# A hybrid decoder step on one core: the memory attention of the sample tokens is paced by other numbers, and the first memory weight tile is rounded in a later call

## The chip, the core and the metric

The kernel runs on one core of a Trainium2 chip. The metric is device time in microseconds (us) of one execution. Three executions of the kernel before took 1181.36, 1183.0 and 1184.02 us. A profile of a further execution shows what each engine did: PE (TensorE, matmuls), PEld (its weight loads), DVE (VectorE), ACT (ScalarE), POOL (GpSimd) and SP, whose queue issues the DMAs.

## The reference

One step of a decoder layer for a prompt of 1024 tokens and eight sample tokens, with shared weights. One input projection feeds three groups of heads: a Mamba-2 state-space group, a dilated window attention, and a cross-attention over 256 memory tokens. Their gated outputs go through one output projection, a residual add and a norm. The part that matters here is the cross-attention, for the prompt with freshly projected memory, for the sample tokens with a cache:

```python
def memory_kv(mem, mem_norm_g, w_mem_kv):
    m = rms_norm(mem, mem_norm_g)
    kv = jnp.einsum('bmd,dn->bmn', m, w_mem_kv)
    k, v = jnp.split(kv, 2, axis=-1)
    return heads(k, CROSS_HEADS), heads(v, CROSS_HEADS)

def cross_attend(q, k, v):
    scale = q.shape[-1] ** -0.5
    sc = jnp.einsum('bthe,bmhe->bhtm', q.astype(F32), k.astype(F32)) * scale
    p = jax.nn.softmax(sc, axis=-1)
    return jnp.einsum('bhtm,bmhe->bthe', p, v.astype(F32))
```

## The kernel before

Products of float32 numbers are made of rounded parts: each operand is split in a high part (`h`, a cast on ACT) and a low part (`l`, a subtraction on DVE or POOL; `split`, L69 to L78), and three matmuls replace one.

The stages in order: q, k and v for all tokens by token tiles (`token_tile`), the memory's keys and values (`memory_tile`, eight tiles of `w_mem_kv`, in between the value tiles), the cross-attention's queries and gates by feature tiles (`feature_tile`: 128 output features, all tokens in three chunks, 24 matmuls each), the prompt's cross-attention, the window attention, the state-space part, and the output projection. `fslot` loads a weight tile of 512 KB into `raw`, one of two buffers, and splits it.

The order of PE's instructions is written out by hand, those of the other engines (and of SP's queue) by a scheduler. PE's order comes from generators that `step` advances: each matmul group yields a cost in ns, and `spend` adds it to a clock, `now`. Background generators are advanced when that clock has passed what they yielded last. `settle` (called at the end of the cross-attention stage, before its buffers are given back) runs whatever the background still holds at once, with no other matmul between.

One background generator is `samples`: the sample tokens' window attention, and then their memory attention, both in `sample_attention`. Of the memory attention (names ending in m: `prm`, `ktm`), for each of eight tokens and two sets of 128 memory rows, a key tile `kt` is loaded (L390), multiplied with the query on DVE (L391) and reduced per head (L392); each of these 16 steps yields 2100 ns, and 6000 ns follow. Then the scores are transposed on PE (`sTm`, L399), the softmax is made, its result transposed back (`sPm`, L432), and 16 value tiles of 256 KB are multiplied on PE (`som`, L464) in four groups of four. Value tiles share five buffers with the key tiles: the first five are loaded ahead, the others as each group gives its buffers back (`load_v`, L449). After each half DVE masks the results (L474), and `sfom` (L480, eight small products in float32) sums them; its first half needs only the first masks.

In the program around it PE works at four gate tiles (`gates`, names `gc`) and then at tiles of z. A gate's end is ACT's tanh (L349), DVE's product (L350), POOL's product with the attention result (L355), and a store of 512 KB to `cat_d` (L358) on SP.

Of the kernel before, what the change touches and what calls it, by code (L numbers as in the profile page):

```python
# [12 lines left out]
F32R = mybir.dt.float32r  # L13
# [7 lines left out]
P = 128  # L21
# [4 lines left out]
KT = D // P  # L26
# [10 lines left out]
def hybrid_step(ctx: ExitStack, tc: tile.TileContext, i, o):  # L37
# [14 lines left out]
    def bank(tag, name):  # L52
        return phase["pool"].tile([P, 512], F32, tag=tag, name=name, bufs=phase["bufs"][tag])
# [10 lines left out]
    def late(ins):  # L64

        if hold:
            after(hold[0], ins)

    def as32(ap):  # L69
        return ap.bitcast(F32)  # L70

    def split(h, l, src, hi=ACT, lo=POOL, mid=None):

        if hi is ACT:
            ACT.copy(h, src)  # L75
        else:
            hi.tensor_copy(h, src)
        lo.tensor_tensor(l, src, as32(h), op=ALU.subtract)  # L78
# [13 lines left out]
    def open_pool(name, side="left"):  # L92
        guards[name] = tc.tile_pool(name=name, bufs=1, side=side, reuse_waits="tile")
        return guards[name].__enter__()
# [77 lines left out]
    def product():  # L172

        return next(x for x in reversed(nc.cur_bb.bb.instructions) if x.engine == mybir.EngineType.PE)

    def after(product, ins):

        sync = mybir.DependencyInfo(mybir.DependencyClass.Sync, mybir.DependencyReason.DATA)
        tc.add_manual_dep(ins.ins, product.name, sync, reason="pace")
# [9 lines left out]
    w2_ = open_pool("w2", "right")  # L189
# [26 lines left out]
    def wslot(name, cols, start=None, pieces=range(4)):  # L216
        out = []
        for j in pieces:
            off, src = 0, []
            for c0, n in cols:  # L220
                src.append((i["w_in"][256 * j:256 * j + 256, c0:c0 + n], off))
                off += n
            out.append(wpiece(f"{name}{j}", src, off, start))
        return out

    def tok_major(ps, slot, xh, xl, n=512, middle=None):


        for kt in range(KT):
            if kt == KT // 2 and middle:  # L230
                middle()
            wh, wl = (t[:, kt % 2, :n] for t in slot[kt // 2])
            PE.matmul(ps, lhsT=xh(kt), rhs=wh, start=(kt == 0), stop=False)  # L233
            PE.matmul(ps, lhsT=xh(kt), rhs=wl, start=False, stop=(kt == KT - 1 and not xl))  # L234
            if xl:
                PE.matmul(ps, lhsT=xl(kt), rhs=wh, start=False, stop=(kt == KT - 1))
            spend(640.0 if xl else 427.0)

    low = [DVE]

    def fslot(name, c0, n=P, w=None, start=None):

        raw = w2_.tile([P, KT, P], F32, tag="fraw", name="raw_" + name, bufs=2)[:, :, :n]
        load = SP.dma_start(raw, (i["w_in"] if w is None else w)[:, c0:c0 + n].rearrange("(k p) n -> p k n", p=P))
        if start:
            after(start, load)
        h = w2_.tile([P, KT, P], F32R, tag="fwh", name="wh_" + name, bufs=2)[:, :, :n]
        l = w2_.tile([P, KT, P], F32R, tag="fwl", name="wl_" + name, bufs=2)[:, :, :n]
        split(h, l, raw, lo=low[0])
        return h, l  # L250

    q_d = dram.tile([S, 512], F32, tag="q_d", name="q_d")

# [62 lines left out]
    def rope(out, x, n, c, s, eng):  # L316

        t = xp_.tile([P, 4, 8, 8], F32, tag="ropet", name="ropet")[:n]
        cb, sb = (v.unsqueeze(1).to_broadcast([n, 8, 8]) for v in (c, s))
        x1, x2 = x[:, :, 0:8], x[:, :, 8:16]  # L320
        eng.tensor_tensor(t[:, 0], x1, cb, op=ALU.mult)
        eng.tensor_tensor(t[:, 1], x2, sb, op=ALU.mult)
        eng.tensor_tensor(t[:, 2], x2, cb, op=ALU.mult)
        eng.tensor_tensor(t[:, 3], x1, sb, op=ALU.mult)
        eng.tensor_tensor(out[:, :, 0:8], t[:, 0], t[:, 1], op=ALU.subtract)
        eng.tensor_tensor(out[:, :, 8:16], t[:, 2], t[:, 3], op=ALU.add)

    def feature_tile(name, c0, done, m=P, lead=0):


        def work(wh, wl):
            for c in range(3):
                cs = slice(c * CH - (lead if c else 0), (c + 1) * CH)
                ps = bank("acc", f"{name}_{c}")[:m, :cs.stop - cs.start]
                for kt in range(KT):
                    PE.matmul(ps, lhsT=wh[:, kt], rhs=hTh[:, kt, cs], start=(kt == 0), stop=False)  # L336
                    PE.matmul(ps, lhsT=wl[:, kt], rhs=hTh[:, kt, cs], start=False, stop=False)  # L337
                    PE.matmul(ps, lhsT=wh[:, kt], rhs=hTl[:, kt, cs], start=False, stop=(kt == KT - 1))  # L338
                    if kt == KT - 1:
                        done(ps, c, cs)  # L340
                    yield 437.0
        add(name, lambda: fslot(name, c0, m), lambda slot: work(*slot))
# [35 lines left out]
    def sample_attention(b_, name, H, sets, q_rows, rows_k, rows_v, scale, new, out):  # L378
# [6 lines left out]
        for b in range(NB):  # L385
            qb = wide("qb", 2)
            SP.dma_start(qb, q_rows[b:b + 1].to_broadcast([P, 512]))
            for s_ in range(sets):
                kt, pr = wide("kt", 5), wide("pr", 2)
                late(SP.dma_start(kt, rows_k(b, s_)))  # L390
                DVE.tensor_tensor(pr, kt, qb, op=ALU.mult)  # L391
                DVE.tensor_reduce(sc[:, s_, b], pr.rearrange("p (h d) -> p h d", h=H), axis=AX.X, op=ALU.add)  # L392
                yield 2100.0
        yield 6000.0
        W = sets * P + (NB if new else 0)
        st = t_([R, W], "st")
        for s_ in range(sets):
# [19 lines left out]
        mx, l, r = t_([R, 1], "mx"), t_([R, 1], "l"), t_([R, 1], "r")  # L417
# [38 lines left out]
        for g in range(2):  # L456
            POOL.memset(om[g], 0.0)
            for s_ in range(sets):
                if s_ == 0:
                    ob = bank("o", f"so{name}{g}")  # L460
                n = 4 * (g * sets + s_)
# [37 lines left out]
    def samples():  # L499
        yield from sample_attention(sa_, "w", 8, 3, qs_d, win(wk), win(wv), 0.125, (o["win_k_s"], o["win_v_s"], 3.0), oAs)  # L500
        while "qc3" not in finished:
            yield 1000.0
        yield from sample_cross(sa_)
# [7 lines left out]
    def join(out, ps, low):  # L511

        DVE.tensor_copy(out[:2 * NB], ps[:2 * NB])
        SP.dma_start(low, out[NB:2 * NB])
        DVE.tensor_tensor(out[:NB], out[:NB], low, op=ALU.add)

    def token_tile(name, T, out, row, middle=None):
        n = P if T < NT else NB
        cs = slice(T * P, T * P + n)
        ps = bank("acc", f"{name}{T}")  # L520
        t = xp_.tile([P, 512], F32, tag="qkv", name=f"{name}sb{T}", bufs=2)
        if T < NT:
            tok_major(ps, slot, lambda kt: hTh[:, kt, cs], lambda kt: hTl[:, kt, cs], middle=middle)
            DVE.tensor_copy(t, ps)
        else:
            tok_major(ps[:2 * NB], slot, lambda kt: hTs[:, kt], None)
            join(t, ps, xp_.tile([P, D], F32, tag="xsq", name=f"{name}low")[:NB, :512])
            t = t[:NB]
        if name != "v":
            c, s = (cos[:, T], sin[:, T]) if T < NT else (cos_s, sin_s)  # L530
            v = t.rearrange("p (h d) -> p h d", h=8)
            rope(v, v, n, c, s, POOL)
        SP.dma_start(out[cs] if T < NT else row, t)
        finished.add(f"{name}{T}")

    def memory_tile(f, slot):
        wh, wl = slot
        ps = bank("acc", f"mem{f}")[:, :256]
        for kt in range(KT):
            PE.matmul(ps, lhsT=wh[:, kt], rhs=mth[:, kt], start=(kt == 0), stop=False)  # L540
            PE.matmul(ps, lhsT=wl[:, kt], rhs=mth[:, kt], start=False, stop=False)
            PE.matmul(ps, lhsT=wh[:, kt], rhs=mtl[:, kt], start=False, stop=(kt == KT - 1))
        t = xp_.tile([P, 512], F32, tag="qkv", name=f"mkv{f}", bufs=2)[:, :256]
        DVE.tensor_copy(t, ps)
        SP.dma_start(o["mem_k" if f < 4 else "mem_v"][:, f % 4], t)
        spend(2600.0)
# [73 lines left out]
    for T in (0, NT, *range(1, NT)):  # L620
        token_tile("k", T, o["win_k"], o["win_k_s"])
        if T == 5:
            start = product()
        if T == 0:
            norm_start("m1")
        elif T in (2, 4):
            norm_end(f"m{T // 2 - 1}")
    slot = wslot("v", [(C_V, 512)])
    mem_w = [fslot("m0", 0, w=i["w_mem_kv"], start=start)]
    for T in (0, NT, *range(1, NT)):  # L630
        token_tile("v", T, o["win_v"], o["win_v_s"])
        if T < NT:
            if T < NT - 1:
                mem_w.append(fslot(f"m{T + 1}", P * (T + 1), w=i["w_mem_kv"], start=product()))
            memory_tile(T, mem_w.pop(0))
# [957 lines left out]
```

## Time and profile before

| what | value |
|---|---|
| median of three executions | 1183.0 us (1181.36 to 1184.02) |
| the profiled execution | 1182.3 us, its span 1180.5 us |
| busy in the span | PE 1107.3, PEld 950.8, DVE 720.1, ACT 477.8, POOL 393.7 us |
| moved by DMA | 137.45 MB, mean 116 GB/s |
| mean granted PE clock | 0.987 of full speed |

The span is the time from the first to the last instruction that the profiler shows. Idle time of an engine counts only where it lies on the chain that ends last. All durations below come from the one profiled execution.

### The profile page before, as it was taken

To read this page: it belongs to the slowest core of one execution; us is meant where nothing else is said; L and a number is where in the kernel's file an instruction comes from. 1 tells how busy PE (TensorE), PEld (TensorE's weight loads), DVE (VectorE), ACT (ScalarE), POOL (GpSimd) and SP (SyncE) were. 2 spreads that over 40 slices of the span, in tenths; PEclk is the share of its full clock that TensorE was granted. 3 is DMA by queue.
4 is the path that set the end of the run, shared out by engine and by line. 5 is a ranking of instruction groups with operands and counts; after the bars stand their busy time and mean duration, and the time that the engine had idled before them with its cause. 6 is when DMAs were issued, how large, how long until landed. Compare 5 with 4: busy or idle time off the path is not lost.

```text
span 1180.5 us, 19065 instructions
## 1 busy us (share of the span) xinstructions
PE 1107.3 (94%) x7059; PEld 950.8 (81%) x7059; DVE 720.1 (61%) x1524; ACT 477.8 (40%) x1156; POOL 393.7 (33%) x422
## 2 busy tenths in 40 slices
PE   7999999999899999999999999998997898998987
PEld 5867676898888888878888899998997777776865
DVE  5558632358842657566664286877858856375663
ACT  5320110244422666565654133555544645214121
POOL 2355200000134205143323411554534325361871
PEclk9999999999999999999999899999998999999999
DMA  5658547613547422121201321112213333363732
GB/s 196 216 162 262 155 117 210 196 45 113 156 143 207 130 76 88 39 76 55 76 21 44 116 93 39 36 41 69 76 51 99 110 96 118 133 201 126 267 128 74
DMA packets 133149, 137.45 MB, mean 116 GB/s; under 512 B 12440, under 2 KB 98984, under 8 KB 133056
## 3 DMA queue, kind: packets, MB, share of 16 engines
q1 hardware_dynamic: 133056, 136.23, 37.4%
q8 instruction: 56, 0.92, 0.3%
q14 instruction: 37, 0.30, 0.1%
HBM read 106.64 MB, written 29.48 MB: 115 GB/s over the span
## 4 chain that ended last, share of the span: by engine, by line
PE 62%; DVE 12%; DMA 11%; issue 5%; ACT 5%; POOL 4%; SPq 1%; DVEq 0%; POOLq 0%; ACTq 0%
PE op L1347 8%; PE conv L336 4%; PE conv L337 4%; PE conv L338 4%; PE pT L862 3%; PE o L877 3%; PE sc L843 2%; PE sc L842 2%; DMA rsb<-rs_d 1%; PE v L233 1%; PE y L1175 1%; PE qc L336 1%; PE v L234 1%; PE ga L336 1%; PE qc L338 1%
## 5 line engine op out<-in xcount | busy, mean ns | idle before, releaser
L336 PE MATMUL conv<-hTh,wh_conv 128*128 128x348 f32 (+1 forms) x384 | 130.1, 339 | 10.9 <-DVE xc L1086 8.0
L337 PE MATMUL conv<-hTh,wl_conv 128*128 128x348 f32 (+1 forms) x384 | 123.8, 322 | 0.0
L338 PE MATMUL conv<-hTl,wh_conv 128*128 128x348 f32 (+1 forms) x384 | 123.6, 322 | 0.0
L1347 PE MATMUL op<-owh,ofwh 128*128 128x512 f32 x256 | 104.4, 408 | 8.0 <-DVE yo L1354 4.9
L849 ACT ACTIVATE p<-p,ml 128x128 f32<-128x128 f32 (+1 forms) x192 | 84.9, 444 | 62.3 <-DVE ml L847 61.7
L1347 PE MATMUL op<-owl,ofwh 128*128 128x512 f32 x256 | 100.7, 393 | 3.3 <-DVE owl L78 3.3
L1086 DVE SCALAR_TENSOR_TENSOR xc<-conv,conv_w,xc 128x341 f32<-128x341 f32 (+2 forms) x144 | 81.8, 568 | 31.9 <-ACT xc L1083 29.4
L1347 PE MATMUL op<-owh,ofwl 128*128 128x512 f32 x256 | 100.6, 393 | 0.0
L336 PEld LDWEIGHTS conv<-hTh,wh_conv 128*128 128x128 f32 x384 | 72.8, 190 | 16.1 <-issue 13.7
L847 DVE CUSTOM_DVE_ANT_0 p<-sc,mask 128x128 f32<-128x128 f32 (+1 forms) x192 | 59.3, 348 | 33.8 <-PE sc L843 24.8
L337 PEld LDWEIGHTS conv<-hTh,wl_conv 128*128 128x128 f32 x384 | 72.8, 190 | 1.5
L338 PEld LDWEIGHTS conv<-hTl,wh_conv 128*128 128x128 f32 x384 | 72.8, 189 | 0.0
L863 DVE COPY pt<-pT 128x256 f32<-128x256 f32 (+1 forms) x96 | 52.1, 544 | 32.2 <-PE pT L862 31.6
L336 PE MATMUL z<-hTh,wh_z 128*128 128x344 f32 x192 | 66.6, 347 | 1.2 <-DVE z L372 1.2
L1347 PEld LDWEIGHTS op<-owh,ofwh 128*128 128x128 f32 x256 | 48.6, 190 | 23.1 <-issue 7.3
L1197 POOL TENSOR_TENSOR cx<-cx,xc 128x512 f32<-128x512 f32 x32 | 43.8, 1370 | 62.4 <-ACT cx L1194 62.4
L78 POOL TENSOR_TENSOR wl_conv<-raw_conv,wh_conv 128x1024 fp32r<-128x1024 f32 x16 | 38.5, 2404 | 78.4 <-ACT wh_conv L75 78.4
L338 PE MATMUL z<-hTl,wh_z 128*128 128x344 f32 x192 | 61.3, 319 | 0.0
L337 PE MATMUL z<-hTh,wl_z 128*128 128x344 f32 x192 | 61.3, 319 | 0.0
L1347 PEld LDWEIGHTS op<-owl,ofwh 128*128 128x128 f32 x256 | 48.5, 190 | 13.8 <-DVE owl L78 4.1
L1347 PEld LDWEIGHTS op<-owh,ofwl 128*128 128x128 f32 x256 | 48.4, 189 | 10.3
L842 PE MATMUL sc<-kk,q 128*128 128x128 f32 (+1 forms) x192 | 55.7, 315 | 0.0
(447 smaller groups left out, 3143.1 us busy)
## 6 DMA issues: line engine op xcount, KB each, us to landing
raw_conv<-w_in SPq DMA_DIRECT2D x16, 512.0 KB
oraw<-w_out SPq DMA_DIRECT2D x16, 512.0 KB
oct<-cat_d SPq DMA_DIRECT2D x16, 512.0 KB
ktw<-cache_win_k SPq DMA_DIRECT2D x24, 256.0 KB
ktw<-cache_win_v SPq DMA_DIRECT2D x24, 256.0 KB
x<-x_prompt SPq DMA_DIRECT2D x8, 512.0 KB
raw_m<-w_mem_kv SPq DMA_DIRECT2D x8, 512.0 KB
ktm<-cache_mem_k SPq DMA_DIRECT2D x16, 256.0 KB
```

Of the source, the lines that this page charges most:

```text
L78: lo.tensor_tensor(l, src, as32(h), op=ALU.subtract)
L336: PE.matmul(ps, lhsT=wh[:, kt], rhs=hTh[:, kt, cs], start=(kt == 0), stop=False)
L337: PE.matmul(ps, lhsT=wl[:, kt], rhs=hTh[:, kt, cs], start=False, stop=False)
L338: PE.matmul(ps, lhsT=wh[:, kt], rhs=hTl[:, kt, cs], start=False, stop=(kt == KT - 1))
L842: PE.matmul(sc[:, h, :w], lhsT=qs_(q[h]), rhs=ks_(kk[h]), start=True, stop=False)
L847: DVE.tensor_tensor_reduce(out=p[:, :w], in0=sc[:, h, :w], in1=mask, scale=-0.125, scalar=HUGE, op0=ALU.add, op1=ALU.min, accum_out=mx)
L849: ACT.activation(p[:, :w], p[:, :w], AF.Exp, scale=-1.0, bias=mx, accum_out=den)
L862: PE.transpose(tp[:, h, t * P:(t + 1) * P], p[:, t * P:(t + 1) * P], ident)
L863: DVE.tensor_copy(pt[:, :, :k * P], tp[:, :, :k * P])
L1086: DVE.scalar_tensor_tensor(xc[:, here.start + cut:here.stop], ps[:, at + cut - 3 + k:at + n - 3 + k], cw[:, ft, k:k + 1], xc[:, here.start ...
L1197: POOL.tensor_tensor(cx, cx, Ct[:, halves[b]], op=ALU.mult)
L1347: PE.matmul(ps[n], lhsT=x[:, kt], rhs=w, start=(kt == 0 and j == 0), stop=(kt == 7 and j == len(parts) - 1))
```

## The change

Two edits. The memory attention of the sample tokens yields 3200 ns for each key product in place of 2100, and 3000 ns behind them in place of 6000 (the window attention keeps its numbers). And `fslot` can be held: it issues the load, and hands back a function that allocates the rounded tiles and splits; for the first memory tile that function is called behind the first value tile, not ahead of it.

```diff
-    def fslot(name, c0, n=P, w=None, start=None):
+    def fslot(name, c0, n=P, w=None, start=None, held=False):
 
         raw = w2_.tile([P, KT, P], F32, tag="fraw", name="raw_" + name, bufs=2)[:, :, :n]
         load = SP.dma_start(raw, (i["w_in"] if w is None else w)[:, c0:c0 + n].rearrange("(k p) n -> p k n", p=P))
         if start:
             after(start, load)
-        h = w2_.tile([P, KT, P], F32R, tag="fwh", name="wh_" + name, bufs=2)[:, :, :n]
-        l = w2_.tile([P, KT, P], F32R, tag="fwl", name="wl_" + name, bufs=2)[:, :, :n]
-        split(h, l, raw, lo=low[0])
-        return h, l
+
+        def parts():
+            h = w2_.tile([P, KT, P], F32R, tag="fwh", name="wh_" + name, bufs=2)[:, :, :n]
+            l = w2_.tile([P, KT, P], F32R, tag="fwl", name="wl_" + name, bufs=2)[:, :, :n]
+            split(h, l, raw, lo=low[0])
+            return h, l
+        return parts if held else parts()
...
-                yield 2100.0
-        yield 6000.0
+                yield 2100.0 if new else 3200.0
+        yield 6000.0 if new else 3000.0
...
-    mem_w = [fslot("m0", 0, w=i["w_mem_kv"], start=start)]
+    mem_w = [fslot("m0", 0, w=i["w_mem_kv"], start=start, held=True)]
     for T in (0, NT, *range(1, NT)):
         token_tile("v", T, o["win_v"], o["win_v_s"])
+        if T == 0:
+            mem_w[0] = mem_w[0]()
```

What the edits do to the orders is seen from the built programs (the change's line numbers are 3 to 5 higher). The DVE instructions of L391 and L392 stand at the same row numbers of DVE's list in both, those of the memory stage among them, and SP's loads of key tiles too. The ACT cast and the DVE subtraction of the first memory tile keep their rows as well. All lists are alike up to the first transposes of the memory scores, `sTm`.

On PE, the last groups of the value products before (`gc` is the last gate's third chunk, `z` the first tile behind it):

```order
L338 MATMUL gc_2_3513<-hTl,wh_gc_3288 128x344
L464 MATMUL som_3464<-ktm,ptm 4x512 x4
L336 MATMUL gc_2_3513<-hTh,wh_gc_3288 128x344
L337 MATMUL gc_2_3513<-hTh,wl_gc_3289 128x344
...
L338 MATMUL z_0_3553<-hTl,wh_z_3437 128x344
L480 MATMUL sfom<-selbm,prm 128x4 x8
L336 MATMUL z_0_3553<-hTh,wh_z_3437 128x344
```

and the same place of the change:

```order
L341 MATMUL gc_2_3471<-hTl,wh_gc_3268 128x344
L467 MATMUL som_3476<-ktm,ptm 4x512 x4
L339 MATMUL gc_2_3471<-hTh,wh_gc_3268 128x344
...
L341 MATMUL z_0_3517<-hTl,wh_z_3386 128x344
L467 MATMUL som_3476<-ktm,ptm 4x512 x4
L467 MATMUL som_3538<-ktm,ptm 4x512 x8
L483 MATMUL sfom<-selbm,prm 128x4 x8
L339 MATMUL z_0_3517<-hTh,wh_z_3386 128x344
```

Before, the four groups of four stand apart among the gates' matmuls, and this is the fourth. In the change the first group stands here, and groups two to four and `sfom` follow each other behind the first three matmuls of z.

On SP's queue, the value tiles and what is issued around them, before (`cat_d` is a gate's store, `raw_z` a weight tile):

```order
L449 DMA ktm<-cache_mem_v 128x512 x8
L358 DMA cat_d<-cacc_2906 128x8x128
L244 DMA raw_z_3702<-w_in 128x8x128
L449 DMA ktm<-cache_mem_v 128x512 x3
L358 DMA cat_d<-cacc_3108 128x8x128
L244 DMA raw_z_4515<-w_in 128x8x128
L59 DMA mask_3577<-mask 128x256
```

and in the change:

```order
L361 DMA cat_d<-cacc_2887 128x8x128
L244 DMA raw_z_3702<-w_in 128x8x128
L452 DMA ktm<-cache_mem_v 128x512 x6
L361 DMA cat_d<-cacc_3084 128x8x128
L452 DMA ktm<-cache_mem_v 128x512 x5
L244 DMA raw_z_4515<-w_in 128x8x128
L59 DMA mask_3577<-mask 128x256
```

The third gate's store and a weight tile go ahead of the eleven later value tiles, and the last gate's store stands between the sixth and the seventh of them.

On ACT, behind the last gate, before (`tz` is the tanh of a chunk of z, `selw`, `qs` and `ks` are casts for the window attention):

```order
L75 CAST wh_z_3698<-raw_z_3696 128x1024
L370 ACTIVATE tz_3635<-z_0_3553 128x344
L748 CAST selw<-selw_raw 128x1024
L772 CAST qs_00_3606<-qt_3598 128x4x2x64
L370 ACTIVATE tz_3663<-z_1_3638 128x344
L774 CAST ks_00_3607<-kt_3599 128x1024
```

and in the change:

```order
L75 CAST wh_z_3698<-raw_z_3696 128x1024
L753 CAST selw<-selw_raw 128x1024
L777 CAST qs_00_3606<-qt_3598 128x4x2x64
L779 CAST ks_00_3607<-kt_3599 128x1024
L373 ACTIVATE tz_3635<-z_0_3517 128x344
L373 ACTIVATE tz_3663<-z_1_3638 128x344
```

The three casts have moved ahead of both tanhs. Much later, in the state-space part, some neighbours change places on ACT, DVE and POOL.

## Rows read from the trace of the kernel before

**Rows 1.** The page: busy time by engine, and the chain that ended last.

```profile
PE 1107.3 (94%) x7059; PEld 950.8 (81%) x7059; DVE 720.1 (61%) x1524; ACT 477.8 (40%) x1156; POOL 393.7 (33%) x422
...
PE 62%; DVE 12%; DMA 11%; issue 5%; ACT 5%; POOL 4%; SPq 1%; DVEq 0%; POOLq 0%; ACTq 0%
```

**Rows 2.** Busy time by stretch: length, engines, PE clock, DMA share, GB/s.

```profile
290.00:300.00 10.00, 7.30 (x54) 7.02 (x53) 10.00 (x26) 4.89 (x13) 0.00 (x0) 1.00 0.61 193
...
310.00:320.00 10.00, 7.46 (x52) 6.45 (x51) 9.93 (x22) 4.29 (x13) 3.24 (x4) 1.00 0.39 109
```

**Rows 3.** The tile prm: ns shortest/median/longest, first and last start.

```profile
L391 DVE TENSOR_TENSOR prm<-ktm,qbm x16: 675/686/693, 281.4 to 314.8; 128x512 f32<-128x512 f32 x16
```

**Rows 4.** Timeline of PE, 340 to 368 us: start, us, instruction.

```profile
340.23 1.04 PE L464 MATMUL som<-ktm,ptm 128*4 128x512 f32 x8
...
346.58 1.04 PE L464 MATMUL som<-ktm,ptm 128*4 128x512 f32 x8
...
352.96 1.40 PE L464 MATMUL som<-ktm,ptm 128*4 128x512 f32 x8
...
359.66 2.52 PE L464 MATMUL som<-ktm,ptm 128*4 128x512 f32 x8
...
365.06 0.32 PE L336 MATMUL z<-hTh,wh_z 128*128 128x344 f32 x1
...
365.53 1.84 PE L480 MATMUL sfom<-selbm,prm 128*128 128x4 f32 x16
367.23 0.41 PE L336 MATMUL z<-hTh,wh_z 128*128 128x344 f32 x1
```

**Rows 5.** Timeline of SP's queue, 341 to 372 us.

```profile
341.28 0.82 SPq L449 DMA_DIRECT2D ktm<-cache_mem_v  x2
...
353.20 0.38 SPq L358 DMA_DIRECT2D cat_d<-cacc  x1
...
354.30 2.30 SPq L449 DMA_DIRECT2D ktm<-cache_mem_v  x3
...
369.89 0.38 SPq L244 DMA_DIRECT2D raw_z<-w_in  x1
...
371.96 0.38 SPq L747 DMA_DIRECT2D selw_raw<-selw  x1
```

**Rows 6.** Busy time of 354 to 360 us, columns as above.

```profile
354.00:360.00 6.00, 6.00 (x36) 5.35 (x37) 1.03 (x2) 0.92 (x2) 0.95 (x2) 1.00 1.00 297
```

**Rows 7.** Timeline of PE's weight loads, the last wait of the fourth group.

```profile
361.15 0.09 PEld L464 LDWEIGHTS som<-ktm,ptm 128*4 128x4 f32 x2 [0.55 <-DMA ktm<-cache_mem_v]
```

**Rows 8.** Timelines of DVE and POOL, 360 to 368 us.

```profile
362.22 2.79 DVE L474 TENSOR_TENSOR prm<-som,hmm 4x512 f32<-4x512 f32 x4 [2.32 <-PE som L464]
...
366.41 0.90 POOL L355 TENSOR_TENSOR cacc<-cacc,gg_x 128x336 f32<-128x336 f32 x1 [5.52 <-DVE gg_x L350]
```

**Rows 9.** The chain of waits, two loads: start, us.

```profile
70.19 4.22 DMA raw_v<-w_in
...
170.84 7.39 DMA ktw<-cache_win_v
```

**Rows 10.** Timelines of PE and ACT, 376 to 380 us.

```profile
379.51 0.43 PE L336 MATMUL z<-hTh,wh_z 128*128 128x344 f32 x1 [1.18 <-DVE z L372]
...
376.99 1.05 ACT L748 CAST selw<-selw_raw 128x1024 fp32r<-128x1024 f32 x1 [5.71 <-DMA selw_raw<-selw]
```

**Rows 11.** Busy time in stretches of 2 us, columns as in Rows 2.

```profile
292.00:294.00 2.00, 0.33 (x3) 0.36 (x4) 2.00 (x7) 0.11 (x2) 0.00 (x0) 1.00 0.61 161
...
938.00:940.00 2.00, 0.10 (x2) 0.09 (x1) 2.00 (x5) 0.52 (x1) 1.15 (x1) 1.00 0.85 315
940.00:942.00 2.00, 2.00 (x19) 1.75 (x21) 1.72 (x2) 2.00 (x7) 0.00 (x0) 0.66 0.90 288
942.00:944.00 2.00, 2.00 (x19) 1.67 (x16) 1.54 (x2) 0.95 (x3) 1.27 (x1) 0.50 0.69 240
```

**Rows 12.** Timeline of PE, 930 to 940 us.

```profile
939.91 0.50 PE L1347 MATMUL op<-owl,ofwh 128*128 128x512 f32 x1 [1.90 <-DVE owl L78]
```

## The prediction

> **What bounds the kernel now.** The page's busy shares and its chain come first: TensorE (PE) is busy 94% of a span of 1180.5 us and carries 62% of the chain [rows 1]. So a change is worth what it takes from, or adds to, PE's waits where PE works through its list. Next come the stretches in which the sample tokens' products of the memory keys run: the 16 products of L391 stand between 281.4 and 314.8 us [rows 3], and from 290 to 300 us VectorE (DVE) is busy 10.00 of 10.00 us while PE has only 7.30 [rows 2]. That is the place that a wider spread could relieve. Third, the timeline of PE from 340 to 368 us [rows 4]: the four groups of value products (`som`) stand some 6.4 us apart between gate matmuls, with start times 340.23, 346.58, 352.96 and 359.66, then the first three matmuls of z from 365.06 to 365.53, the last small products `sfom`, and z again at 367.23. PE hardly waits there. Fourth, the loads that feed these groups, on SP's queue [rows 5].
>
> **The changed yields.** The generator is stepped by a clock of written costs, but only PE's list follows it directly. The orders of the change show what became of it: all 32 DVE instructions of L391 and L392 of the memory stage stand at the same places of DVE's list, their key loads at the same places of SP's. Nothing is spread, so I count no gain in 290 to 320 us. What does move is PE's part behind the products: 16 steps are now worth 51.2 us instead of 33.6 and the pause behind them 3.0 instead of 6.0, 14.6 us later in all. The gates end before that time is spent. Group one comes four chunks of a gate tile later, and groups two to four and `sfom` fall behind the first three matmuls of z, back to back, with no matmul between them.
>
> **Held memory weights.** The rounding of the first memory tile is called behind the first value tile, but its ACT cast and DVE subtraction keep their places among the others, and the load stays put on SP. Zero; all of 0 to 326 us is then as before. If a hidden wait differed, it would show as a changed time of the first memory matmul.
>
> **Term 1, the value groups back to back.** Without groups two to four ahead of it (1.04, 1.40 and 2.52 us [rows 4]; the row's time is about what each costs PE), z begins at 365.06 - 4.96 = 360.10, and group two follows after 0.47 us, at 360.57. There are 16 value tiles of 256 KB in five buffers. Group two uses tiles 5 to 8; their loads start behind group one, some 5 us before, and should be nearly there. Loads 10 to 16 can only be issued as groups two and three release buffers. SP's first such issue stands 1.05 us behind a group's start (340.23 to 341.28, [rows 4, 5]), here 361.62. The last gate's store to cat_d (512 KB) stands between them on SP; it waits for POOL's last gate product, which ended at 367.31 [rows 8] and comes some 5 us earlier. So 7 x 0.262 + 0.524 = 2.36 MB go through one queue. The rate there is 297 GB/s with the DMA engines full [rows 6], so 7.95 us. The nearest like it in the trace, one such store, one weight tile and three value tiles (1.83 MB, 6.18 us at that rate), took from 353.20 to the end of the last wait at 361.15 [rows 5, 7], 7.95 us, so 1.77 us come on top. The last tile lands at 361.62 + 7.95 + 1.77 = 371.34. From there, as in the trace, 1.07 us to DVE's masking (361.15 to 362.22), four of them in 2.79 us [rows 8], and the second half of `sfom`, 0.9 us of 1.84 [rows 4]: z resumes at 376.1 instead of 367.23, **+8.9 us**. In between PE has only the 12 short products and half of `sfom`.
>
> Bounds: a chain that no bandwidth can shorten is two loads long, since load 16 takes the buffer of tile 11, which is itself loaded behind group two. A 512 KB load alone took 4.22 us [rows 9]; less 0.88 us for the missing half at 297 GB/s, 3.34 us for 256 KB. Then tile 11, issued 0.41 us behind the first, lands at 365.37, load 16 goes out 1.05 us later and lands at 369.76, and z resumes at 374.5, +7.3. At the other end one value load in company took 7.39 us [rows 9]; twice that gives 382.6, +15.4. I take 8.9, as the row of 353 to 361 us holds the very same transfers.
>
> The row of a load alone is 4.22 us for 512 KB [rows 9]. The Trainium skill, page "DMA: Bandwidth & Descriptors", section "Anatomy of one DMA — SWDGE (gpsimd) path", gives about 2.0 us fixed plus bytes at 436 GB/s, stated for another issuing path; by estimate 3.2 us for 512 KB, 2.6 for 256 KB, and term 1 would be +5.8 in place of +8.9. The trace does not agree with it here.
>
> **Term 2, what is late next.** After the first tile of z, before, PE waited 1.18 us for DVE to clear the second chunk's bank, behind ACT, which stood at the cast of `selw`, ahead of that chunk's tanh, until its load had landed: issued at 371.96, cast at 376.99 [rows 5, 10]. SP now reaches these loads when load 16 is out, about 366.6 us, and the weight load ahead of them stood at 369.89 before [rows 5]: some 3 us earlier, while z is 9 us later. Though ACT now has three casts ahead of z's first tanh, all should be done before PE is. **-1.2 us**; between -1.2 and 0.
>
> **Term 3, the clock.** Behind a wait of PE from 938 to 940 us (0.10 us busy) the granted clock was 0.66 and then 0.50 in the next two stretches of 2 us [rows 11], between its two levels, 2.4 and 1.2 GHz: 0.34 x 2 + 0.50 x 2 = 1.7 us lost. In 292 to 294, with 0.33 us busy, it stayed at 1.00 [rows 11]. Here PE is nearly idle for 15 us, so I take **+2.0**, between 0 and 3.4 (two falls).
>
> **Term 4, 930 to 950 us.** The scheduler also exchanges neighbours on ACT, DVE and POOL in the last part. PE waits 1.90 us there for a DVE subtraction (`owl`) [rows 12], and the new order takes one short instruction from ahead of it; the casts that it puts later on ACT serve products that PE needs only 9 us on. At best the wait goes, -1.9; I take 0, since the cast ahead of the subtraction still waits for its load.
>
> **Sum.** 8.9 - 1.2 + 2.0 = 9.7 us on the profiled execution's own 1182.3 us, 1192.0. That execution lies 0.7 us under the median of 1183.0, so I forecast **1192.5 us**. Behind 380 us nothing refunds it: PE's list goes on in the same order and the window stage's loads and casts follow PE's own progress.
>
> **The rivals.** (a) The loads wait for nothing but each other, and the clock holds: 7.3 - 1.2 + 0 = +6.1, 1189.1 us, and 1187.2 if term 4's whole wait goes too. For it: group two's tiles, issued from 341.28 on, were not waited for at 346.58 [rows 4, 5]. Against: the store and a weight tile share the queue. This is also the way of the page's rule above. 0.2. (b) Loads in company take their long time once: a first load of 3.34 and a last of 7.39 make +11.4, with two clock falls 1183.0 + 11.4 - 1.2 + 3.4 = 1196.6, twice long up to 1200. For it: 7.39 us was seen with a 512 KB load behind it, as here. 0.13. (c) Not slower: VectorE is relieved after all. In 290 to 300 us PE lacks 2.7 us, and from 310 to 320 another 2.54 [rows 2]; if the products stepped back there, up to 5.2 us return, and with (a)'s +6.1 the time would be 1183.9. It decides if a single L391 row of the memory stage stands later in DVE's list or its load later in SP's; none does, so it needs a shift that the lists don't hold. 0.05. (d) The moved groups cost nothing, since tiles come in time (1183): PE would have to be back at z by 368.4, before load 16 can even be issued. 0.02.
>
> **How the numbers follow.** The forecast's own cases (1190 to 1195) get 0.6. 0.2% is 2.4 us, about what a measurement tells from no change here. Faster 0.03, same 0.04, slower 0.93. The range from 1187.5 to 1197 leaves out most of (c), (d) and the far end of (b), some 0.13.
>
> **What would show it.** Right: L391 and all else until 326 us at their times; `som` group two near 360 us, groups three and four with waits for ktm of several us each, z again near 376; the 1.18 us wait gone; a lower clock behind 370; later stages shifted by about 10 us. Wrong: PE back at z before 372 us; a changed DVE stretch at 290 us; or PE waits behind 385 us that shrink by as much.

## The result, and the profile after

The changed kernel took 1191.34 us (median of four, 1190.43 to 1195.09), the kernel before on the same chip 1182.18 (four, 1181.2 to 1184.02): a ratio of 1.0077, 95% interval 1.0060 to 1.0094. It is slower by 9.2 us. The profiled execution of the change took 1190.43 us, 8.1 more than that of before (1182.3); its span is 1188.6. Two of the twelve executions of pool_mul, one of the kernels below, took 2777 and 3666 us and are left out of its ratio.

The page of the change, busy time and chain, against [rows 1]; and the tile prm, against [rows 3]:

```profile
PE 1111.3 (93%) x7059; PEld 951.7 (80%) x7059; DVE 717.2 (60%) x1524; ACT 477.7 (40%) x1156; POOL 394.4 (33%) x422
...
PE 61%; DVE 13%; DMA 12%; ACT 5%; issue 4%; POOL 3%; SPq 1%; DVEq 0%; POOLq 0%; ACTq 0%
```

```profile
L394 DVE TENSOR_TENSOR prm<-ktm,qbm x16: 673/676/692, 282.1 to 315.5; 128x512 f32<-128x512 f32 x16
```

The 16 key products take 33.4 us from the first to the last start, as before, both ends 0.7 us later, as the work ahead of them already is. Nothing was spread. The granted clock fell there in the change (0.50 from 296 to 298 us) and not in before, but from the first key product to z's first matmul, groups two to four taken off, it is 78.4 us in the change and 78.7 in before, so that fall cost nothing. What did move shows in the timeline of PE, 360 to 376 us, against [rows 4]:

```profile
360.49 0.32 PE L339 MATMUL z<-hTh,wh_z 128*128 128x344 f32 x1
...
361.05 2.85 PE L467 MATMUL som<-ktm,ptm 128*4 128x512 f32 x10
364.96 1.84 PE L467 MATMUL som<-ktm,ptm 128*4 128x512 f32 x4 [1.06 <-DMA ktm<-cache_mem_v]
368.00 4.12 PE L467 MATMUL som<-ktm,ptm 128*4 128x512 f32 x10 [1.19 <-DMA ktm<-cache_mem_v]
372.05 1.05 PE L483 MATMUL sfom<-selbm,prm 128*128 128x4 f32 x8
375.09 1.02 PE L483 MATMUL sfom<-selbm,prm 128*128 128x4 f32 x8 [1.99 <-DVE prm L477]
375.97 0.40 PE L339 MATMUL z<-hTh,wh_z 128*128 128x344 f32 x1
```

Twenty-four short products (two passes for each of 12 tiles) and `sfom` stand alone between z's first three matmuls and its return at 375.97, which was 367.23. Each product's weights are loaded first, and there the waits are seen, in the timeline of PE's weight loads (three of eight waits):

```profile
365.78 0.09 PEld L467 LDWEIGHTS som<-ktm,ptm 128*4 128x4 f32 x2 [0.73 <-DMA ktm<-cache_mem_v]
368.00 0.09 PEld L467 LDWEIGHTS som<-ktm,ptm 128*4 128x4 f32 x2 [2.12 <-DMA ktm<-cache_mem_v]
...
371.09 0.09 PEld L467 LDWEIGHTS som<-ktm,ptm 128*4 128x4 f32 x2 [0.65 <-DMA ktm<-cache_mem_v]
```

On SP's queue, against [rows 5], six value loads go out as buffers come free, then the last gate's store, then five more, then a weight tile (for z's fifth tile) and the window stage's `selw`, whose cast on ACT no longer stands in PE's way (last row, ACT):

```profile
357.15 5.76 SPq L452 DMA_DIRECT2D ktm<-cache_mem_v  x6
363.00 0.38 SPq L361 DMA_DIRECT2D cat_d<-cacc  x1
363.49 3.67 SPq L452 DMA_DIRECT2D ktm<-cache_mem_v  x5
367.21 0.43 SPq L244 DMA_DIRECT2D raw_z<-w_in  x1
...
368.83 0.64 SPq L752 DMA_DIRECT2D selw_raw<-selw  x1
```

```profile
374.87 1.04 ACT L753 CAST selw<-selw_raw 128x1024 fp32r<-128x1024 f32 x1 [12.79 <-DMA selw_raw<-selw]
```

Busy time by stretch (columns as in [rows 2]); the clock is the third number from the right:

```profile
366.00:372.00 6.00, 4.79 (x12) 0.45 (x10) 0.00 (x1) 0.00 (x0) 2.31 (x3) 1.00 1.09 361
...
376.00:378.00 2.00, 2.00 (x11) 2.00 (x11) 0.39 (x2) 1.49 (x2) 1.43 (x2) 0.66 1.22 290
378.00:380.00 2.00, 2.00 (x9) 2.00 (x8) 0.00 (x0) 0.00 (x0) 1.09 (x1) 0.50 1.22 290
380.00:382.00 2.00, 2.00 (x14) 2.00 (x13) 0.41 (x1) 0.46 (x1) 0.00 (x0) 0.99 1.21 295
```

Behind the idle stretch the granted clock fell to 0.50, the lower of its two levels: 0.34 x 2 + 0.50 x 2 + 0.01 x 2 = 1.7 us. The first transpose of the window stage starts at 390.82 instead of 381.99, 8.8 us later; at the kernel's end 8.1 us of that are left.

### The profile page after: what moved, and what is told of

Same layout as the page of the kernel before. It is cut to its first block, busy times and chain, and to the rows that moved or that the text cites. A ratio compares the mean times of both kernels' runs of the same rounds, so it can differ in the third digit from the quotient of the medians.

```text
span 1188.6 us, 19067 instructions
## 1 busy us (share of the span) xinstructions
PE 1111.3 (93%) x7059; PEld 951.7 (80%) x7059; DVE 717.2 (60%) x1524; ACT 477.7 (40%) x1156; POOL 394.4 (33%) x422
## 4 chain that ended last, share of the span: by engine, by line
PE 61%; DVE 13%; DMA 12%; ACT 5%; issue 4%; POOL 3%; SPq 1%; DVEq 0%; POOLq 0%; ACTq 0%
PE op L1352 7%; PE conv L339 4%; PE conv L340 4%; PE conv L341 4%; PE pT L867 3%; PE o L882 3%; PE sc L848 2%; PE sc L847 2%; PE z L339 2%; PE z L341 2%; PE z L340 2%; DMA qbw<-qs_d 2%; DMA rsb<-rs_d 1%; PE ga L339 1%; PE qc L339 1%
```

## The experiments

Eleven kernels were run, one of them twice, each beside the kernel before on its own chip. Three columns of the table come from the one profiled execution of each: how long z is interrupted (from the start of its first matmul to the start of its fourth), the time from the first key product to the first `cb` matmul of the state-space stage (456.1 us before), which leaves out both what happens ahead of 280 us and what happens behind 740, and the second wait for `owl` near 940 us [rows 12]. In fill and pool_fill groups stand among z's matmuls, and in the other pool runs z is interrupted as in before (2.17 to 2.18). Falls of the clock stand in the columns too: `sfom`'s second half, 0.9 us from its start to z's return at full clock, takes 0.8 us longer in late10, late15 and no_loads and 0.4 in deep7 and alone; and a fall between 450 and 468 us, which before and the change do not have, takes up to 1.7 us in late5, no_loads, deep7, alone, pool_mul and pool_mul2.

| kernel | ratio to before (95%) | z interrupted | prm to cb | wait for owl |
|---|---|---|---|---|
| before | 1 | 2.17 | 456.1 | 1.90 |
| the change | 1.0077 (1.0060 to 1.0094) | 15.48 | 463.9 | 0.53 |
| late5 | 1.0015 (1.0001 to 1.0028) | 6.25 | 459.0 | 1.53 |
| late10 | 1.0060 (1.0036 to 1.0083) | 14.06 | 463.4 | 0.53 |
| late15 | 1.0081 (1.0062 to 1.0099) | 16.74 | 465.7 | 0.53 |
| fill | 0.9998 (0.9981 to 1.0014) | | 457.0 | 0.54 |
| no_loads | 1.0007 (0.9991 to 1.0024) | 9.13 | 458.6 | 1.83 |
| pe_busy | 1.0071 (1.0046 to 1.0097) | 16.29 | 462.2 | 1.68 |
| deep7 | 1.0069 (1.0042 to 1.0095) | 16.71 | 467.5 | 2.07 |
| alone | 1.0085 (1.0060 to 1.0111) | 14.79 | 465.5 | 1.92 |
| pool_mul | 0.9959 (0.9936 to 0.9982) | | 454.1 | 0.59 |
| pool_mul2 | 0.9967 (0.9948 to 0.9985) | | 456.2 | 0.62 |
| pool_deep7 | 0.9948 (0.9925 to 0.9971) | | 454.3 | 1.11 |
| pool_fill | 1.0013 (0.9992 to 1.0033) | | 458.7 | none |

**The sum alone: late15, late10, late5.** Without either edit, only the pause behind the products grows (to 11.0, 15.8 and 20.6):

```diff
-        yield 6000.0
+        yield 6000.0 if new else 11000.0
```

> The kernel before, with the pause behind the memory products lengthened from 6.0 to 20.6, so that the sum of the written costs is the change's own; the spacing of 2100 and the early rounding of the memory weights stay. Theory: only the sum decides, three groups fall behind z as in the change, 1191.3 us within 1.5. Rival (spacing or rounding matter by themselves): the time falls back towards 1182 by what they are worth.

> The kernel before, with the pause behind the memory products lengthened from 6.0 to 15.8: two value groups (the third and fourth) fall behind the first three matmuls of z. Theory (each group that is pulled together leaves its loads less time): group four's tiles 14 to 16 can only be asked for as group three releases buffers, so PE waits some 4 us for the last of them, then 3 to 4 us for masking and the last products; 1185 to 1188 us, between the 1183.0 with one group and the 1191.5 with three. Rival (one more wait of 1 to 2 us for each group, evenly): 1184.5.

> The kernel before, with the pause behind the memory products lengthened from 6.0 to 11.0 and nothing else: one value group (the fourth) instead of three falls behind the first three matmuls of z. Theory (what costs is that groups behind the last gate have no matmul between them): group four then starts at once behind group three's gates and z, and DVE's masking (2.79 us) and the last small products are no longer covered; z resumes some 2 to 3 us later than before, 1184 to 1186 us. Rival one (the 3.2 spacing of the products or the held rounding is what costs): 1182, as before. Rival two (any later group costs the same at once): near 1191.

late15 measured 1191.5 us, and its ratio is the change's within the noise of some 2 us: by themselves the spacing of the products and the held rounding are worth nothing that can be told, and the rival falls. late5 measured 1182.99, 0.15% or 1.8 us above before, and late10 1188.64, 0.6% or 7 us; the expectations, counted from 1183.0, had 1 to 3 and 2 to 5 us. The loss is not even by group. Take off the groups that stood ahead of z before (1.04 to 2.52 us each, [rows 4]): z's interruption grows by 1.6 us with one group behind it, by 8.0 with two, by 8.4 in the change and 9.6 in late15 with three (of the 8.0 and the 9.6, 0.8 is the lower clock). PE's timeline of late5, the fourth group and what follows:

```profile
364.75 1.83 PE L464 MATMUL som<-ktm,ptm 128*4 128x512 f32 x8
366.51 1.05 PE L480 MATMUL sfom<-selbm,prm 128*128 128x4 f32 x8
369.55 1.02 PE L480 MATMUL sfom<-selbm,prm 128*128 128x4 f32 x8 [1.99 <-DVE prm L474]
```

One group finds its loads asked for by the group before; it waits 0.70 us for one of them and pays mainly for the masking, 1.99 us. With two, the last three loads can only be asked for inside the idle stretch, from 363.68 us on.

**The loads left out: no_loads.**

```diff
+                if n >= 5 and not new:
+                    tiles[n] = tiles[n - 5]
+                    return
                 tiles[n] = wide("kt", 5)
```

> The changed kernel without the loads of the memory value tiles 6 to 16: their products read the first five tiles again, so the sample tokens' cross-attention values are left out from there. Order and number of PE's instructions stay. Theory (the loads are the term): PE's waits for ktm, 8 to 9 us together between 361 and 371, go; the wait for DVE's masking ahead of the last small products stays; z resumes near 368 instead of 375.97, and the time is 1182 to 1185 us. Rival (the masking and the short products themselves set it): z resumes not before 372, 1187 us or more.

1183.08 us, and PE's timeline:

```profile
359.24 2.76 PE L470 MATMUL som<-ktm,ptm 128*4 128x512 f32 x24
363.29 1.03 PE L486 MATMUL sfom<-selbm,prm 128*128 128x4 f32 x8 [1.29 <-DVE prm L480]
366.11 1.84 PE L486 MATMUL sfom<-selbm,prm 128*128 128x4 f32 x8 [1.79 <-DVE prm L480]
367.81 0.63 PE L339 MATMUL z<-hTh,wh_z 128*128 128x344 f32 x1
```

The same 24 products take 2.76 us; z returns at 367.81 as expected, and the interruption falls by 6.4 us. So the loads are the larger part of it; 2.0 us beyond before's remain, 0.8 of them the lower clock under `sfom`'s second half (1.84 us instead of 1.02), the rest the masking that nothing covers.

**Matmuls in between: fill.**

```diff
     until("gc3")
+    while background and step():
+        pass
     settle()
```

> The changed kernel, but where its groups are emitted back to back behind the last gate, the steps of z are taken instead for as long as there are any (8 or 9 us of them), and groups two and three come among them when they are due. Theory: the load waits of groups two and three are covered; group four and the last small products still stand alone behind z's tile, 4 to 5 us, and that tile no longer covers the start of the window stage: 1183 to 1189 us, PE's waits for ktm between 360 and 372 gone. Rival (it is the lateness of the groups that costs): no better than 1191.

1181.31 us, at before's time and better than I expected. Groups two and three stand 6.4 us apart among z's matmuls and wait for nothing (PE's timeline); group four and `sfom` still stand together behind the tile:

```profile
361.78 1.04 PE L467 MATMUL som<-ktm,ptm 128*4 128x512 f32 x8
...
368.14 1.04 PE L467 MATMUL som<-ktm,ptm 128*4 128x512 f32 x8
...
373.56 1.58 PE L467 MATMUL som<-ktm,ptm 128*4 128x512 f32 x8
...
378.11 1.31 PE L483 MATMUL sfom<-selbm,prm 128*128 128x4 f32 x8 [1.99 <-DVE prm L477]
```

The groups are as late as in the change, so lateness isn't the loss: standing back to back is. Up to `cb` 6.9 of the change's 7.8 us are gone. That the total is even with before's goes with a second thing, the shorter wait for `owl` (below).

**PE kept busy: pe_busy.** Matmuls that nobody reads stand in the waits:

```diff
+                    keep({9: 8, 11: 8, 14: 3}.get(n + c, 0))
...
+            keep(8 * g)
```

> The changed kernel with 27 matmuls more on PE, of 128x512 elements into a bank that nobody reads: 8, 8 and 3 of them in the waits ahead of value tiles 10, 12 and 15 and 8 ahead of the second half of the last small products, where PE waits some 2 us each. Theory (the load waits are the loss, and some 1.7 us of it a fall of the clock behind them): z still resumes at 375 to 377 us, the granted clock stays at 1.00 from 372 to 382, and the time is 1 to 2 us below the change's, 1189 to 1190.5. Rival (the fall of the clock costs nothing or comes whatever PE does): 1191, or more by what the added matmuls take.

1188.14 us. z's interruption is 0.8 us longer than the change's, but the clock never falls there:

```profile
376.00:378.00 2.00, 2.00 (x15) 2.00 (x14) 0.13 (x1) 0.00 (x0) 0.00 (x0) 1.00 1.26 298
```

From z's return to the first transpose of the window stage it takes 13.28 us (375.47 to 388.75), the change 14.85 (375.97 to 390.82), before 14.76 (367.23 to 381.99). So the fall costs 1.57 us, and before's wait of 1.18 us [rows 10] was worth 1.48. In the total the ratio, 1.0071, can't be told from the change's.

**Buffers or company: deep7 and alone.** deep7 lends the value tiles two buffers (`wide("qb", 2)` for two tiles of seven) and loads seven ahead. alone holds the last gate's store, the weight tile behind it and the window stage's loads until the last value product:

```diff
+    after(lastv[0], kept[0]())
+    hold.append(lastv[0])
```

> The changed kernel with seven buffers for the memory value tiles instead of five (the two of the query rows, qb, are free by then and serve as the sixth and seventh), so that seven loads stand ahead and a group's products release four of them for tiles seven further on. Order and number of the products stay. Theory (the loss is loads that can only be asked for as buffers come free): behind z's first matmuls only five loads of 256 KB are left to ask for instead of seven, the last lands near 368 instead of 371.09, z resumes near 373 and the time is 2 to 4 us below the change's 1191.3, 1187 to 1189.5 us. Rival (the bytes in company with the store and the weight tile set it, whenever they are asked for): z still resumes near 376 and the time stays within 1 us of the change's.

> The changed kernel, but the store of the last gate's tile to cat_d, the weight tile behind it and the loads of the window stage wait for the last value product, so that the last eleven value loads stand alone on the DMA engines; five buffers as in the change. The run with seven buffers left two loads fewer to ask for, and yet its last tile landed at the same 371 us, with the DMA engines full from 364 on. Theory now (bytes in company: the 512 KB store ahead of the last five loads and the weight tile behind them): the last value tile lands at 368 to 369.5 instead of 371.09 and z resumes at 372.5 to 374.5 instead of 375.97; of the total some may be lost again to the window stage's loads, which start 4 us later. Rival (the chain of loads that wait for buffers sets it, whatever else is on the engines): the last value tile at 370.5 or later, z at 375.5 or later.

deep7 measured 1189.96 us. Its last product's weights still wait until 371.00 (timeline of PE's weight loads), 10.01 us behind group two's start, in the change 10.04:

```profile
368.83 0.09 PEld L468 LDWEIGHTS som<-qbm,ptm 128*4 128x4 f32 x2 [3.11 <-DMA qbm<-cache_mem_v]
...
371.00 0.09 PEld L468 LDWEIGHTS som<-ktm,ptm 128*4 128x4 f32 x2 [1.42 <-DMA ktm<-cache_mem_v]
```

So the theory that the number of buffers sets it fell, as far as buffers alone go, and I formed another, the bytes in company. The run alone speaks on that one. The last value tile is there at 370.15 (timeline of PE's weight loads), 8.93 us behind group two's start, and the engines then lie idle:

```profile
370.15 0.09 PEld L470 LDWEIGHTS som<-ktm,ptm 128*4 128x4 f32 x2 [0.56 <-DMA ktm<-cache_mem_v]
```

```profile
370.00:372.00 2.00, 2.00 (x12) 0.99 (x10) 0.78 (x2) 0.00 (x0) 0.00 (x0) 1.00 0.00 0
```

That is between the two expectations and nearer to the rival: with company away, 8.93 of the 10.04 us remain.

The two runs together show two limits that lie close to each other. In the change the path is the chain of loads that wait for buffers: tile 11's weights are loaded at 365.78, and the load that takes its buffer goes out 1.05 us later, here with the weight tile behind it (timeline of SP's queue). That last tile is there at 371.09.

```profile
366.83 0.33 SPq L452 DMA_DIRECT2D ktm<-cache_mem_v  x1
367.21 0.43 SPq L244 DMA_DIRECT2D raw_z<-w_in  x1
```

In deep7 the last three loads follow the store one behind another and wait for no product, so this chain is gone; yet the last tile takes until 371.00, with the DMA engines full (busy share 0.96) at 287 GB/s (SP's queue, and busy time by stretch):

```profile
363.41 0.53 SPq L452 DMA_DIRECT2D qbm<-cache_mem_v  x1
364.03 2.09 SPq L452 DMA_DIRECT2D ktm<-cache_mem_v  x2
366.22 0.44 SPq L244 DMA_DIRECT2D raw_z<-w_in  x1
...
366.00:371.00 5.00, 2.82 (x7) 0.18 (x5) 0.00 (x0) 0.00 (x0) 2.31 (x3) 0.85 0.96 287
```

late10 has no such chain either: its last load goes out behind the store at 365.05, and its tile is there at 370.42. So either remedy alone meets the other limit, 371.00 by the bytes in company or 370.15 by the chain, and neither can gain more than 1 us. How low the bytes would come without the weight tile, which deep7 asks for 1 us earlier, is open, and the two remedies together were not tried. In total alone took 1192.55 us, no gain: behind z's return PE works through the change's own list, 2.3 us slower up to `cb`, at a clock that stays low until 381.4 us instead of 380.1 and falls once more from 463 to 467.

**VectorE relieved: pool_mul, pool_mul2, pool_fill, pool_deep7.** The stretch that rival (c) spoke of, on the kernel before (GpSimd, POOL, is idle in the first of the two stretches only, [rows 2]):

```diff
-                DVE.tensor_tensor(pr, kt, qb, op=ALU.mult)
+                (DVE if new else POOL).tensor_tensor(pr, kt, qb, op=ALU.mult)
```

> The kernel before with one edit: the 16 products of the memory keys run on GpSimd instead of VectorE. VectorE is full from 290 to 300 and 310 to 320 us while GpSimd is idle there, and PE waits 5.0 us for the scaling of cp and 1.4 us for cptl between 281 and 320 us. Theory (VectorE's fill is what holds PE there, and the change didn't touch it): 10.9 us less on VectorE, up to 6 us of PE's waits go, 1176 to 1180 us. Rival (GpSimd and VectorE slow each other, or the sums then wait for GpSimd and hold VectorE's list): 1181.4 or more.

> The kernel before with the memory key products on GpSimd, the same kernel as the run of that edit alone, beside the one with seven buffers on the same chip. If VectorE's fill is the cause, again 3 to 6 us below the kernel before, with PE's waits for cp and cptl between 281 and 320 us near 4.6 us instead of 6.4; if the first verdict was chance, no difference.

> The edit of the products on GpSimd together with the emission of z's steps between the late groups, on the kernel before with its own spacing. If both theories hold, the last small products stand within z and the gain of the GpSimd edit is kept or bettered by up to 1 us: 1175 to 1180 us. If the emission costs later what it saves here, no better than the GpSimd edit alone.

> The kernel before with its own spacing, the memory key products on GpSimd and seven buffers for the memory value tiles. In the run with the GpSimd edit alone group four took 2.70 us instead of the 1.04 of an unwaiting group. If both hold, group four falls to 1.04 to 1.5 us and the time is 1 to 1.7 us below that edit alone; if the wait only moves to the loads behind it, the same.

pool_mul measured 1178.14 us and the same kernel again 1178.91: ratios of 0.9959 and 0.9967, faster than both kernels of this study. In pool_mul, in 290 to 300 us PE is busy 9.76 instead of 7.30 [rows 2], and from 281 to 320 it waits 4.6 us for `cp` and `cptl` where the same groups of before show 6.4 (5.0 and 1.4):

```profile
290.00:300.00 10.00, 9.76 (x70) 9.05 (x68) 9.45 (x23) 5.14 (x14) 7.76 (x7) 1.00 0.71 214
```

```profile
L703 PE MATMUL co<-cptl,mvh 128*128 128x256 f32 x20 | 5.8, 290 | 2.6 <-DVE cptl L78 2.6
L690 PE MATMUL cpT<-ident,cp 128*128 128x128 f32 x36 | 5.5, 274 | 2.0 <-DVE cp L683 2.0
```

The same window holds more work in pool_mul (20 `co` products of a kind instead of 16), so the two waits are no measure of the gain. From prm to cb the gain is 2.0 us in one profile and nothing in the other, where a clock fall in 302 to 310 us took 3.4 us. Both have the short wait for `owl`, which by itself can be worth as much. How much of the 4 us is VectorE's relief stays open. pool_deep7 measured 1175.35, ratio 0.9948, the fastest of all; its fourth group still takes some 2 us, and its interval overlaps pool_mul's, so that the two buffers help isn't shown. pool_fill gained nothing: z's tile is spent among the groups, and PE then waits 3.60 us near 389 us for the window stage's cast of q on DVE, where pool_mul has 0.66.

## Why the prediction was right, step by step

**The changed yields, held memory weights.** Right. The products did not move (282.1 to 315.5), and late15, with neither edit, took 1191.5 us.

**Term 1.** Size nearly right, and in part by luck. z returned at 375.97 (376.1 said), and beyond the groups that had stood ahead of z its interruption grew by 15.48 - 2.17 - 4.96 = 8.35 us instead of 8.9. The last tile was there 10.04 us behind group two's start, where the sum had 371.34 - 360.57 = 10.77. The sum priced this as bytes through one queue, at 297 GB/s and 1.77 us on top, and set the chain of two loads aside as a lower bound. The change's last load waited for a buffer, so the path was the chain: without company it takes 8.93 us (alone), where the bound's own chain had 369.76 - 360.57 = 9.19, and company adds 1.1. The price of the bytes is not refuted by this: in deep7, without the chain, they end at 10.01 us. What the sum had wrong is which of the two the change waits for, and the rate, 361 GB/s from 366 to 372 us; its size holds because the two limits lie within some 1 us. The estimate from the Trainium skill's page "DMA: Bandwidth & Descriptors", section "Anatomy of one DMA — SWDGE (gpsimd) path", +5.8, stays too low also for loads without company: alone gives 14.79 - 2.17 - 4.96 = +7.7, 0.4 of it the lower clock.

**Term 2.** -1.2 predicted, -1.48 measured (by pe_busy, above). The wait is gone; `selw`'s load was issued at 368.83 and not by 366.6, its cast was at 374.87 instead of 376.99, in time.

**Term 3.** +2.0 predicted, +1.57 measured, one fall of the clock.

So up to the first window transpose the three terms make 8.35 - 1.48 + 1.57 = 8.4 us; the sum had 9.7.

**Term 4.** Taken as 0, and wrong. The wait of 1.90 us [rows 12] became 0.53, and the clock, which fell behind it before [rows 11], stayed at 1.00, another 1.7 us. PE's timeline of the change:

```profile
948.17 0.50 PE L1352 MATMUL op<-owl,ofwh 128*128 128x512 f32 x1 [0.53 <-DVE owl L78]
```

In the change, late10, late15, fill, pool_mul and pool_mul2 this wait is 0.53 to 0.62 us, and no clock fall follows by 956 us; in before, late5, no_loads, pe_busy, deep7 and alone it is 1.53 to 2.07, with a fall each time. Two things tell the two sets apart. In the first the `st` update (0.41 us) runs behind the `owl` subtraction that PE waits for, in the second ahead of it. And a small subtraction ahead of both, `oxs`, takes 0.21 or 0.22 us in all of the first set and 1.31 or 1.32 in all of the second, where POOL's product `cx` runs beside it. Timelines of DVE and POOL, before:

```profile
936.53 1.31 DVE L78 TENSOR_TENSOR oxs<-catAXs,oxs 128x64 fp32r<-128x64 f32 x1
```

```profile
936.18 1.58 POOL L1197 TENSOR_TENSOR cx<-cx,xc 128x512 f32<-128x512 f32 x1 [5.01 <-ACT cx L1194]
```

and the change, where `cx` comes 2.3 us behind it:

```profile
946.17 0.21 DVE L78 TENSOR_TENSOR oxs<-catAXs,oxs 128x64 fp32r<-128x64 f32 x1
```

```profile
948.47 1.27 POOL L1202 TENSOR_TENSOR cx<-cx,xc 128x512 f32<-128x512 f32 x1 [0.26 <-ACT cx L1199]
```

1.10 + 0.41 us make 1.51; the wait lost 1.37. No run has one of the two without the other. The prediction saw the exchange of neighbours and allowed up to -1.9 for the `st` update; it took 0 because the cast ahead of the subtraction still waits for its load, and that reason did not hold. That a POOL product holds up VectorE was not in its rows.

The 3.1 us did not stay: from cb to the end the change took 442.6 us and before 443.0. PE's order is the same in both there, so the matmuls can be matched one by one. The change loses 1.2 us at a wait for `xc` near 900 us, is 1.8 us ahead behind `owl` and the clock, and 0.4 ahead behind a wait for `yo` near 1085 us. PE's timelines, before and the change:

```profile
894.58 0.62 PE L336 MATMUL conv<-hTh,wh_conv 128*128 128x344 f32 x1 [6.47 <-DVE xc L1086]
...
1083.61 0.47 PE L1347 MATMUL op<-owh,ofwh 128*128 128x512 f32 x1 [1.73 <-DVE yo L1354]
```

```profile
904.32 0.62 PE L339 MATMUL conv<-hTh,wh_conv 128*128 128x344 f32 x1 [7.67 <-DVE xc L1091]
...
1090.24 0.76 PE L1352 MATMUL op<-owh,ofwh 128*128 128x512 f32 x1 [3.68 <-DVE yo L1359]
```

In the other runs these two waits take 3.8 to 7.7 and 3.0 to 3.7 us; what sets them was not traced. So the total, 1191.3 against 1192.5, was met by the terms up to 390 us (8.4 for 9.7), and behind that by things that were not foreseen and nearly cancelled, which is luck.

**The rivals.** (a) named the path that the change took, loads that wait for each other, but its sum without company and with the clock held, 1189.1, lies below all four executions of the change; (b) and (d) didn't come. (c)'s condition wasn't met; the stretch that it named may hold something all the same, if VectorE's work is really taken away.

## What to carry to other kernels

A number that paces a background task is read by what it pushes past the next point where everything left is run at once: look there first, and at whether loads that are asked for only as buffers come free still have work of another kind in front of them, and what else shares the DMA engines with them. Here one group pushed over that point cost 1.6 us, two some 7. Where such a point can't be avoided, let it take steps of the next stage in between (fill gave back 6.9 of 7.8 us), but count what that stage then lacks at its start (pool_fill). And when an edit exchanges neighbours in a far stage, look at what runs on POOL beside VectorE's short work there: 1.1 us on one subtraction here, in a wait that a fall of the clock followed.

## What was not expected of the hardware

Some of VectorE's work between SBUF buffers is held up while POOL works. Term 4 shows it in the kernel as it was: 0.21 us became 1.31 beside a POOL product. pool_mul, where POOL takes 1.29 us for a key product that took VectorE 0.69, shows it on few instructions. Of 16 scalings of `cp` two took 0.94 and 1.38 us beside a POOL product and the others 0.34 to 0.35, as in before; of seven short ones of `cmx` three took 0.56 to 0.61, where before has one of 0.31 and else at most 0.17; a weight tile's subtraction took 1.67 instead of 1.23. So the mean of the scalings rose from 349 to 448 ns while their median stayed. The reductions of `prm`, most of them beside a POOL product too, kept their time (mean 678 ns in both), and so did work that reads PSUM (`cptl` 686 and 681). VectorE from 281 to 316 us, ns shortest/median/longest, the scalings in before and in pool_mul, then the reductions in pool_mul:

```profile
L683 DVE TENSOR_SCALAR cp<-cp,cmx x13: 337/350/358, 286.0 to 316.0; 128x256 f32<-128x256 f32 x13
```

```profile
L683 DVE TENSOR_SCALAR cp<-cp,cmx x16: 341/348/1378, 281.2 to 315.1; 128x256 f32<-128x256 f32 x16
...
L392 DVE TENSOR_REDUCE scm<-prm x16: 662/677/689, 282.8 to 311.5; 128x4 f32<-128x512 f32 x16
```

The Trainium skill, page "Perfetto Trace Analysis", section "Optimizing Scalar/DVE Operations", says that the two engines share a read port to SBUF, which some of VectorE's operations hold for themselves, so that moving work from one to the other might not help. The trace agrees that there is a price, up to 1.0 us on a scaling of 0.35 and 1.1 us on one small subtraction; the kernel with the move was still faster in both runs.
